# A block product scheme for the last down projection, widened from 36 to 40 of 44 input tiles and cut into two sets

## The chip, the core and the metric

The kernel runs on one core of a Trainium2 chip. The metric is device time in microseconds (us), as the median of three runs. TensorE (PE in the profile) multiplies matrices into PSUM, VectorE (DVE) and ScalarE (ACT) work element by element, GpSimd (POOL) here issues transfers that add in memory, and SyncE (SP) issues the loads of weights. PE's weight loads (PEld) run beside its matmuls.

## The reference

Two layers of an encoder over 272 tokens (16 learned ones and 256) with 2048 channels, all in float32. Each layer ends in a feed-forward block with 5632 inner channels:

```
h2 = rmsnorm(h)
up = h2 @ w_up                                     # 2048 -> 2 * 5632
act = silu(dwconv3(up[:, :5632])) * up[:, 5632:]   # conv over tokens
h  = h + act @ w_down                              # 5632 -> 2048
return h[16:]                                      # after the last layer
```

The change is in `act @ w_down` of the second layer: 256 tokens, 5632 inputs (44 tiles of 128), 2048 outputs.

## The kernel before

**Precision.** Every float32 product is made of three matmuls in a reduced form: the weights of each chunk (128 x 1024 values, 512 KB) are split by `split_w` into `wh`, a cast on ScalarE (L253), and `wl`, what the cast left out, a subtraction on VectorE (L256). Activations are split likewise (`split_to`, L1209 and L1210). Then high x high, low x high and high x low are summed in PSUM.

**The order.** `order` lists all weight chunks in the order of use. `load_raw` issues their loads on SP's queue some chunks ahead, `next_split` brings the split two chunks ahead of use (`LOOK`), and `wh` and `wl` have three buffers each. `group` (L325 to L327 for the gate half `ps_ug`, L321 and L322 for the value half `ps_uv`) multiplies one group of 256 up-projection channels: 4 chunks for the gate half, then 4 for the value half. In the last layer there are 22 such pairs of groups, 176 chunks. After each pair the code of `conv_gate` and of the loop over `UP_ORDER` makes two activation tiles on ScalarE and VectorE (L1196 to L1202, L1344 to L1347).

**The block products.** The last down projection takes `KS` = 36 of the 44 input tiles in a scheme of seven block products for eight: the tokens are cut into two halves, the 36 tiles into two halves of `NQ` = 18, the outputs into two halves of 1024. Each of the seven products `p` = 0 to 6 runs over 18 steps; one step is one weight chunk and six matmuls of 512 columns (`ps_p`, L1305). Products 3 to 6 multiply sums of weight blocks. `weight_sums` has GpSimd's queue make these sums in device memory (`ft`, L514) far ahead, four kinds one after the other over all 18 tiles. The activation operands are made by `make` into two buffers of up to three steps (`opnd`).

`PRODUCTS` fixes the order: products 0 and 4 interleaved by two steps while their activations are being made, then 5, 2, 6, 1 and 3 in full. `due` says how many of the 126 steps stand before each chunk: two steps for each pair of groups (32 in all) up to chunk 144, then 56 over the 32 up chunks of the last four group pairs, then 38 over the first 14 of the 16 tail chunks. Each product has its own pair of PSUM tiles (`open_ps`). When it is finished, `add` puts it into the result `res` in SBUF with a sign (L1271, one for each 512 columns). A sum over several products, which two parts of the output need, is kept in an SBUF tile `usum` (L1318, L1320): it starts as product 0, then products 5 and 6 are added to it.

**The tail.** The other 8 input tiles are multiplied directly: 4 output blocks of 512 (`TAIL_ORDER`), 4 chunks each, 12 matmuls of 512 columns a chunk (`ps_t`, L1379). The last block uses eighteen matmuls a chunk, six of 512 and twelve of 256 columns. Their operands are `tH` and `tL`. A counter `left` says which `add` is the last for a part of `res`; it issues the store of the output.

Of the kernel before, what the change touches and what calls it, by code (L numbers as in the profile page):

```python
# [10 lines left out]
F32 = mybir.dt.float32  # L11
# [5 lines left out]
P = 128  # L17
# [15 lines left out]
CW = 4  # L33
MG = 2
FF_SPLIT = (24, 20)
KS = 36
NQ = KS // 2
UP_ORDER = [i + j * NQ // 2 for i in range(NQ // 2) for j in range(2)] + list(range(NQ, FT // 2))
PRODUCTS = [(p, 2 * i + k) for i in range(NQ // 2) for p in (0, 4) for k in range(2)] + [(p, k) for p in (5, 2, 6, 1, 3) for k in range(NQ)]
TAIL_ORDER = (2, 3, 0, 1)  # L40
F0 = 1536

# [91 lines left out]
def encoder_kernel(ctx, tc, xT, params, consts, bmat, cfold, csign, w_fl, w_f64c, w_in, w_abr, w_four, w_f64, w_out, w_up, w_down, w_dn, w_dt, out):  # L134
# [43 lines left out]
        order.append(((1, "t", b), [(w_dt[b, j], CW) for j in range((FT - KS) // 2)]))  # L178
    prods = {0: w_dn[0, 0:NQ], 1: w_dn[0, NQ:KS], 2: w_dn[1, NQ:KS], 3: ft[3], 4: ft[0], 5: ft[1], 6: ft[2]}
    pchunks = [(prods[p][k], CW) for p, k in PRODUCTS]  # L180
    n_up, n_tail = (FT - KS) // MG * 2 * KT // CW, len(TAIL_ORDER) * (FT - KS) // 2
    n0 = 4 * (NQ // 2 - 1)
    n1 = n0 + 56
    due = lambda t: n0 + 56 * t // n_up if t <= n_up else min(n1 + (len(pchunks) - n1) * (t - n_up) // (n_tail - 2), len(pchunks))
    chunks, folded, mix, summed = [], set(), {}, {}
    t, done = 0, 0
    for key, chs in order:
        for j, ch in enumerate(chs):
            n = 0
            if key[0] == 1 and (key[1] == "t" or key[1] in ("ug", "uv") and key[2] >= KS // MG):  # L190
                n = due(t) - done
                t += 1
            elif key[0] == 1 and key[1] in ("ug", "uv") and key[2] % (NQ // 2) and j == 2:
                n = 1
            if n:
                mix[key, j] = n
                for p, k in PRODUCTS[done:done + n]:
                    if p in (3, 4, 5, 6):
                        summed[len(chunks)] = ((3, 0, 1, 2)[p - 3], k // 2)
                    chunks.append(pchunks[done])  # L200
                    done += 1
                first_mix = min(first_mix, len(chunks) - n) if done > n else len(chunks) - n
            if key[:2] == (0, "s"):
                folded.add(len(chunks))
            chunks.append(ch)
# [300 lines left out]
    def weight_sums():  # L506
        rows = lambda ap: ap.rearrange("k p c m -> (k p) (c m)")
        dst = lambda q, j: rows(ft[q, 2 * j:2 * j + 2])
        w = lambda h, k, j: rows(w_dn[h, NQ * k + 2 * j:NQ * k + 2 * j + 2])

        def issue(q, j, s, **kw):
            tick = small.tile([P, 1], F32, tag="tick", name="tick", bufs=1)
            tc.keep_in_program_order(nc.gpsimd.tensor_copy(tick, st["wl"][:, 0, 0:1].bitcast(F32)))
            tc.keep_in_program_order(nc.gpsimd.dma_start(dst(q, j), s, **kw))  # L514

        for q, base, more in ((0, lambda j: w(0, 0, j), lambda j: w(1, 0, j)),
                              (1, lambda j: dst(0, j), lambda j: w(1, 1, j)),
                              (2, lambda j: w(1, 1, j), lambda j: w(1, 0, j)),
                              (3, lambda j: w(0, 1, j), lambda j: dst(1, j))):
            for j in range(NQ // 2 + 1):  # L520
                if j < NQ // 2:
                    issue(q, j, base(j))
                    yield 1
                if j:
                    issue(q, j - 1, more(j - 1), accum_op=ALU.add, max_dma_last_dim=4096)
                    ready_sums.add((q, j - 1))
                    yield 1

    def norm_stats(holder, gap=0):
        am = small.tile([P, P // NM, NM], F32, tag="am", name="am", bufs=1)  # L530
# [28 lines left out]
    for l in range(DEPTH):  # L559
# [622 lines left out]
        with tc.tile_pool(name=f"ffn{l}", bufs=1) as fp:  # L1182
# [49 lines left out]
                slow[2] = 0  # L1232

            if last:
                KX = KS - KS // 6
                XF = XT.rearrange("p k t -> p (k t)")
                asum = XF[:, 0:NQ * P].rearrange("p (k t) -> p k t", k=NQ)
                acts = ((0, fp.tile([P, KX, SEQ], F32, name="act")),
# [8 lines left out]
                    k0, t_ = acts[k >= KX]  # L1247
                    return t_[:, k - k0:k - k0 + n, tk]

                left = {(h, b): 4 if h == 0 and b > 1 else 3 for h in range(2) for b in range(4)}  # L1250

                def to_tokens():
                    for b in range(4):
# [23 lines left out]
                def make(p, k, n):  # L1277
# [9 lines left out]
                    for q in range(n):  # L1287
                        made[p, k + q] = t_[:, 0, q], t_[:, 1, q]

                def products():  # L1290
                    usum = wp.tile([P, CW, MG * P], F32, tag="wpm", name="usum", bufs=1).rearrange("p c m -> p (c m)")
                    open_ps, late = {}, []
                    for n, (p, k) in enumerate(PRODUCTS):
                        if k == 0:
                            open_ps[p] = [psum.tile([P, 512], F32, tag="aux", name=f"ps_p{p}") for _ in range(2)]
                        ps = open_ps[p]
                        if n >= 2 * NQ - 1 and k % 3 == 1 and n + 2 < len(PRODUCTS):
                            make(*PRODUCTS[n + 2], 3)
                        if n == 2 * NQ - 2:
                            make(*PRODUCTS[2 * NQ], 3)  # L1300
                        wh, wl = (w.rearrange("p c m -> p (c m)") for w in next_split())
                        a, b = made.pop((p, k))
                        for x, w in ((a, wh), (b, wh), (a, wl)):
                            for h in range(2):
                                nc.tensor.matmul(ps[h], x, w[:, 512 * h:512 * h + 512], start=k == 0 and w is wh and x is a,  # L1305
                                                 stop=k == NQ - 1 and w is wl)
                            if x is b or w is wl:
                                step()
                                pump()
                        if late and k % 2 == 0:  # L1310
                            add(*late.pop(0))
                        if k == NQ - 1:
                            while late:
                                add(*late.pop(0))
                            for h in range(2):
                                u_ = usum[:, 512 * h:512 * h + 512]
                                if p == 0:
                                    nc.scalar.copy(u_, ps[h])  # L1318
                                if p in (5, 6):
                                    nc.vector.tensor_tensor(u_, u_, ps[h], op=ALU.add)  # L1320
                            for h in range(2):
                                u_ = usum[:, 512 * h:512 * h + 512]
                                for t_, c, minus in {0: ((0, 0, 0),), 4: ((0, 2, 0), (1, 2, 0)), 5: ((0, 2, 1),),
                                                  2: ((0, 2, 0),), 6: ((1, 0, 0), (1, 2, 1)),
                                                  1: ((0, 0, 0),), 3: ((1, 0, 0),)}[p]:
                                    late.append((t_, c + h, u_ if p in (5, 6) else ps[h], minus))
                            if p in (0, 3):
                                while late:
                                    add(*late.pop(0))
                        yield  # L1330

                st["products"] = products()
                st["pool"] = fp
                for i in UP_ORDER:
# [5 lines left out]
                    for m in range(MG):  # L1340
                        j = 2 * i + m
                        cv = cs[m][:, lo2:T]
                        v = fp.tile([P, W2], F32, tag="v", name="v", bufs=2)
                        nc.scalar.copy(v, ps[m][:, W2:2 * W2])  # L1344
                        nc.vector.tensor_tensor(v, v, ps[m][:, :W2], op=ALU.add)
                        if j < KS:
                            nc.vector.tensor_tensor(act(j, 1, slice(0, SEQ))[:, 0], cv, v, op=ALU.mult)  # L1347
                        else:
                            nc.vector.tensor_tensor(cv, cv, v, op=ALU.mult)
                            split_to(tH[:, j - KS], tL[:, j - KS], cv)  # L1350
                    if i == NQ // 2:
                        until(hold, "tokens")
                    if KS // 2 <= 2 * i < KS:
                        k1, k2 = 2 * i - NQ, 2 * i
                        a21 = act(k1, 2, tk2)
                        nc.vector.tensor_tensor(asum[:, k1:k1 + 2], a21, act(k2, 2, tk2), op=ALU.subtract)
                        nc.vector.tensor_tensor(a21, act(k1, 2, tk1), a21, op=ALU.subtract)
                        for p in (0, 4):
                            make(p, k1, 2)

                for b in TAIL_ORDER:
                    k, chs = order[st["grp"]]
# [4 lines left out]
                    ps = [psum.tile([P, 512], F32, tag="aux" if r == 2 else "mm", name=f"ps_t{r}") for r in range(len(regs))]  # L1367
# [87 lines left out]
```

## Time and profile before

| | before |
|---|---|
| median of 3 runs | 2549.21 us (2548.55 to 2549.77) |
| the profiled execution's own time | 2549.0 us |
| its span in the profile | 2547.2 us |
| PE busy | 2537.5 us (100%) |
| VectorE busy | 1785.9 us (70%) |
| ScalarE busy | 1281.3 us (50%) |
| moved by DMA | 603 MB, mean 237 GB/s |

The profile is of one execution. The span goes from its first to its last instruction; the time has 1.8 us around it. The last feed-forward block begins at about 1820 us. Times in the views are us from the start of the span, durations of single instructions in groups are ns. Matmuls are pipelined: a matmul of 512 columns lasts 390 ns from start to end, and the next starts well before that.

### The profile page before, as it was taken

What the parts mean: (1) busy time and instruction counts of PE and PEld (TensorE: products, weight loads), DVE (VectorE), ACT (ScalarE), POOL (GpSimd) and SP (SyncE); (2) the same over time, 40 slices, a digit from 0 to 9 for tenths busy, and PEclk for the clock granted to TensorE, in tenths of its full rate; (3) what the DMA queues carried; (4) which work ended last, traced back from release to release, by engine and by line L of the source; (5) the groups of instructions that cost most, each with busy time, mean ns of one, the idle gap of its engine ahead of it and who ended that gap; (6) DMA issues with size and microseconds to landing.
All of it is one profiled execution on the core that took longest, in us unless ns stands there. A gap on an engine that the chain in (4) does not pass through costs nothing.

```text
span 2547.2 us, 47579 instructions
## 1 busy us (share of the span) xinstructions
PE 2537.5 (100%) x19160; PEld 2462.4 (97%) x19160; DVE 1785.9 (70%) x2832; ACT 1281.3 (50%) x1842; POOL 86.2 (3%) x185
## 2 busy tenths in 40 slices
PE   9999999999999999999999999999999999999999
PEld 9999999999999999999999999999999999998887
DVE  7687766776666556666559787666766666678787
ACT  5455534554444334444445555444655555556665
POOL 0000000000000000000000000000000000000000
PEclk9999999999999999999999999999999999999999
DMA  6544555688898889898776546775889876668887
GB/s 237 163 155 162 187 181 183 219 245 288 292 289 274 279 285 292 271 297 266 247 226 198 175 149 189 238 216 192 277 257 300 277 241 207 205 211 271 278 297 254
DMA packets 160813, 603.01 MB, mean 237 GB/s; under 512 B 18304, under 2 KB 23552, under 8 KB 160016
## 3 DMA queue, kind: packets, MB, share of 16 engines
q1 hardware_dynamic: 148208, 522.33, 60.7%
q0 software_dynamic: 10944, 75.50, 12.3%
q8 instruction: 150, 2.46, 0.4%
q10 hardware_dynamic: 1440, 2.13, 0.2%
q14 instruction: 71, 0.58, 0.1%
HBM read 578.23 MB, written 94.37 MB: 264 GB/s over the span
## 4 chain that ended last, share of the span: by engine, by line
PE 99%; DVE 1%; DMA 0%; issue 0%; ACT 0%; SPq 0%; POOL 0%; ACTq 0%; DVEq 0%
PE ps_ug L326 7%; PE ps_p L1305 7%; PE ps_ug L327 7%; PE ps_ug L325 7%; PE ps_uv L321 6%; PE ps_d L326 3%; PE ps_uv L326 3%; PE ps_d L325 3%; PE ps_uv L327 3%; PE ps_d L327 3%; PE ps_uv L325 3%; PE ps_uv L322 3%; PE ps_o L326 2%; PE ps_gf L326 2%; PE ps_o L325 2%; PE ps_o L327 2%
## 5 line engine op out<-in xcount | busy, mean ns | idle before, releaser
L256 DVE TENSOR_TENSOR wl<-raw,wh 128x1024 fp32r<-128x1024 f32 (+1 forms) x907 | 1096.6, 1218 | 625.5 <-ACT wh L253 616.0
L253 ACT CAST wh<-raw 128x1024 fp32r<-128x1024 f32 (+1 forms) x907 | 945.9, 1047 | 951.8 <-PE ps_ug L326 170.3
L326 PE MATMUL ps_ug<-xHL,wh 128*128 128x272 f32 (+1 forms) x1408 | 402.0, 286 | 0.0
L327 PE MATMUL ps_ug<-xHL,wl 128*128 128x272 f32 (+1 forms) x1408 | 401.2, 285 | 0.0
L325 PE MATMUL ps_ug<-xHL,wh 128*128 128x272 f32 (+1 forms) x1408 | 401.0, 285 | 0.0
L325 PEld LDWEIGHTS ps_ug<-xHL,wh 128*128 128x128 f32 x1408 | 264.5, 188 | 2.2
L326 PEld LDWEIGHTS ps_ug<-xHL,wh 128*128 128x128 f32 x1408 | 264.7, 188 | 1.5
L327 PEld LDWEIGHTS ps_ug<-xHL,wl 128*128 128x128 f32 x1408 | 264.7, 188 | 0.1
L321 PE MATMUL ps_uv<-xHL,wh 128*128 128x512 f32 x704 | 249.5, 394 | 0.0
L326 PE MATMUL ps_uv<-xHL,wh 128*128 128x272 f32 x704 | 203.3, 289 | 0.0
L326 PE MATMUL ps_d<-gHL,wh 128*128 128x272 f32 x704 | 202.9, 288 | 0.0
L325 PE MATMUL ps_d<-gHL,wh 128*128 128x272 f32 x704 | 202.9, 288 | 0.0
L327 PE MATMUL ps_uv<-xHL,wl 128*128 128x272 f32 x704 | 202.6, 288 | 0.0
L325 PE MATMUL ps_uv<-xHL,wh 128*128 128x272 f32 x704 | 202.3, 287 | 0.0
L327 PE MATMUL ps_d<-gHL,wl 128*128 128x272 f32 x704 | 202.1, 287 | 0.0
L322 PE MATMUL ps_uv<-xHL,wl 128*128 128x256 f32 x704 | 198.4, 282 | 0.3 <-DVE wl L256 0.3
L321 PEld LDWEIGHTS ps_uv<-xHL,wh 128*128 128x128 f32 x704 | 132.1, 188 | 29.6
L325 PE MATMUL ps_ga<-xHL,wh 128*128 128x272 f32 (+1 forms) x512 | 147.8, 289 | 0.0
L325 PE MATMUL ps_gf<-xHL,wh 128*128 128x272 f32 (+1 forms) x512 | 146.7, 287 | 0.0
L326 PE MATMUL ps_o<-mL,wh 128*128 128x272 f32 (+1 forms) x512 | 146.5, 286 | 0.0
L327 PE MATMUL ps_o<-mH,wl 128*128 128x272 f32 (+1 forms) x512 | 146.1, 285 | 0.0
L326 PE MATMUL ps_gf<-xHL,wh 128*128 128x272 f32 (+1 forms) x512 | 146.1, 285 | 0.0
(353 smaller groups left out, 5826.7 us busy)
## 6 DMA issues: line engine op xcount, KB each, us to landing
raw<-in_w_up SPq DMA_DIRECT2D x352, 512.0 KB, 4.8
raw<-in_w_in SPq DMA_DIRECT2D x191, 512.0 KB, 3.9
raw<-in_w_down SPq DMA_DIRECT2D x88, 512.0 KB, 4.8
raw<-ft SPq DMA_DIRECT2D x72, 512.0 KB, 4.7
raw<-in_w_out SPq DMA_DIRECT2D x64, 512.0 KB, 3.6
ft<-in_w_dn POOLq DMA_DIRECT2D x27, 1024.0 KB, 11.9
raw<-in_w_dn SPq DMA_DIRECT2D x54, 512.0 KB, 4.7
raw<-in_w_abr SPq DMA_DIRECT2D x32, 512.0 KB, 3.8
```

The lines of the kernel that those rows point to most:

```text
L253: nc.scalar.copy(h[:, a:b], r[:, a:b])
L256: nc.vector.tensor_tensor(lo[:, a:b], r[:, a:b], h[:, a:b].bitcast(F32), op=ALU.subtract)
L321: nc.tensor.matmul(o2, h[:, c, sl], ab, start=kt == 0, stop=False)
L322: nc.tensor.matmul(o, lo[:, c, sl], ab[:, 0, :], start=False, stop=kt == nk - 1)
L325: nc.tensor.matmul(o, h[:, c, sl], a, start=kt == 0, stop=False)
L326: nc.tensor.matmul(o, h[:, c, sl], b, start=False, stop=False)
L327: nc.tensor.matmul(o, lo[:, c, sl], a, start=False, stop=kt == nk - 1)
L1305: nc.tensor.matmul(ps[h], x, w[:, 512 * h:512 * h + 512], start=k == 0 and w is wh and x is a, stop=k == NQ - 1 and w is wl)
```

## The change

`KS` becomes 40, in two sets of `SETS` = (12, 8) tile pairs. Each set is a complete scheme of seven products over its own tiles, one after the other: 84 steps, then 56. `HOME` says where each activation tile lies in the sets' order; `w_dn` is laid out in that order, and `weight_sums` makes all four kinds of sums for the first set and then for the second. The tail keeps 4 tiles, 2 chunks for each output block, 8 in all.

The steps stand where a written table `DUE` puts them, over all 184 chunks: none before chunk 16, 20 steps over chunks 16 to 96, 64 over 98 to 144, 12 over 144 to 160, 28 over 162 to 176, 16 over the tail chunks 176 to 182.

PSUM holds two pairs of banks, `bank`, for all products. Product 5 is accumulated on top of 0, 6 on top of both and 3 on top of these, and 2 on top of 4; only 0, 4 and 1 start afresh. After each product `add` reads the running sum, and the next product is added to it in place. So `usum` and the addition of products in SBUF go, and each product has two adds to `res`. The two pairs change roles in the second set. The last tail block's third region uses one of these banks.

Operands are made by `make_ahead`: `units` are runs of up to three steps of one product, and when a unit has been multiplied the unit two places later is made.

```diff
-KS = 36
-NQ = KS // 2
+SETS = (12, 8)
+NQ = sum(SETS)
+KS = 2 * NQ
+def _sets():
+    up, prods, home, q0 = [], [], {}, 0
+    for n in SETS:
+        up += [q0 + i + j * n // 2 for i in range(n // 2) for j in range(2)]
+        prods += [(p, q0 + 2 * i + k) for i in range(n // 2) for p in (0, 4) for k in range(2)]
+        prods += [(p, q0 + k) for p in (5, 2, 6, 1, 3) for k in range(n)]
+        for k in range(n):
+            home[2 * q0 + k], home[2 * q0 + n + k] = q0 + k, NQ + q0 + k
+        q0 += n
+    return up + list(range(NQ, FT // MG)), prods, home
+DUE = ((0, 0), (16, 0), (96, 20), (98, 20), (144, 84), (160, 96), (162, 96), (176, 124), (182, 140), (184, 140))
...
-        for q, base, more in (...):
-            for j in range(NQ // 2 + 1):
+        for q0, n in zip(FIRSTS, SETS):
+            for q, base, more in kinds:
+                j0, j1 = q0 // 2, (q0 + n) // 2
+                for j in range(j0, j1 + 1):
...
+                def make_ahead():
+                    while used[1] < min(used[0] + 2, len(units)) and whole.issuperset(units[used[1]][1]):
+                        p, qs = units[used[1]]
+                        make(p, qs[0], len(qs))
+                        used[1] += 1
...
                 def products():
-                    usum = wp.tile([P, CW, MG * P], F32, tag="wpm", name="usum", bufs=1).rearrange("p c m -> p (c m)")
...
-                        if k == 0:
-                            open_ps[p] = [psum.tile([P, 512], F32, tag="aux", name=f"ps_p{p}") for _ in range(2)]
-                        ps = open_ps[p]
-                        if n >= 2 * NQ - 1 and k % 3 == 1 and n + 2 < len(PRODUCTS):
-                            make(*PRODUCTS[n + 2], 3)
+                    bank.extend([psum.tile([P, 512], F32, tag="aux", name=f"ps_p{i}{h}") for h in range(2)] for i in range(2))
+                    for p, q in PRODUCTS:
+                        s = max(i for i, q0 in enumerate(FIRSTS) if q >= q0)
+                        ps = bank[(p in (4, 2, 1)) ^ s % 2]
+                        fresh = p in (0, 4, 1)
...
-                                nc.tensor.matmul(ps[h], x, w[:, 512 * h:512 * h + 512], start=k == 0 and w is wh and x is a,
-                                                 stop=k == NQ - 1 and w is wl)
+                                nc.tensor.matmul(ps[h], x, w[:, 512 * h:512 * h + 512], start=fresh and q in FIRSTS and w is wh and x is a,
+                                                 stop=q in LASTS and w is wl, skip_group_check=not fresh)
...
+                        if units[used[0]][1][-1] == q:
+                            used[0] += 1
+                        make_ahead()
-                        if late and k % 2 == 0:
+                        if late and q % 2 == 0:
                             add(*late.pop(0))
...
-                                if p == 0:
-                                    nc.scalar.copy(u_, ps[h])
-                                if p in (5, 6):
-                                    nc.vector.tensor_tensor(u_, u_, ps[h], op=ALU.add)
...
+                            t_, c, minus = {0: (0, 0, 0), 4: (1, 2, 0), 5: (0, 2, 1), 2: (0, 2, 0), 6: (1, 2, 1), 1: (0, 0, 0), 3: (1, 0, 0)}[p]
+                            late += [(t_, c + h, ps[h], minus) for h in range(2)]
```

More of the change, by code (lines that the diff above doesn't have):

```diff
@@ L35 @@
 FF_SPLIT = (24, 20)
-KS = 36
-NQ = KS // 2
-UP_ORDER = [i + j * NQ // 2 for i in range(NQ // 2) for j in range(2)] + list(range(NQ, FT // 2))
-PRODUCTS = [(p, 2 * i + k) for i in range(NQ // 2) for p in (0, 4) for k in range(2)] + [(p, k) for p in (5, 2, 6, 1, 3) for k in range(NQ)]
+SETS = (12, 8)
[11 more added lines that the diff above has]
+    return up + list(range(NQ, FT // MG)), prods, home
+UP_ORDER, PRODUCTS, HOME = _sets()
+FIRSTS = [sum(SETS[:i]) for i in range(len(SETS))]
+LASTS = [q + n - 1 for q, n in zip(FIRSTS, SETS)]
+DUE = ((0, 0), (16, 0), (96, 20), (98, 20), (144, 84), (160, 96), (162, 96), (176, 124), (182, 140), (184, 140))
 TAIL_ORDER = (2, 3, 0, 1)
@@ L180, in encoder_kernel, with due @@
     pchunks = [(prods[p][k], CW) for p, k in PRODUCTS]
[L181 to L184, printed above, removed]
+    def due(t):
+        (t0, d0), (t1, d1) = next(v for v in zip(DUE, DUE[1:]) if v[0][0] <= t < v[1][0])
+        return d0 + (d1 - d0) * (t - t0) // (t1 - t0)
     chunks, folded, mix, summed = [], set(), {}, {}
@@ L189, in encoder_kernel @@
             n = 0
-            if key[0] == 1 and (key[1] == "t" or key[1] in ("ug", "uv") and key[2] >= KS // MG):
+            if key[0] == 1 and key[1] in ("t", "ug", "uv"):
                 n = due(t) - done
                 t += 1
-            elif key[0] == 1 and key[1] in ("ug", "uv") and key[2] % (NQ // 2) and j == 2:
-                n = 1
             if n:
@@ L514, in issue @@
             tc.keep_in_program_order(nc.gpsimd.dma_start(dst(q, j), s, **kw))
[L516 to L519, printed above, removed]
-            for j in range(NQ // 2 + 1):
[L521 to L527, printed above, removed]
+        kinds = ((0, lambda j: w(0, 0, j), lambda j: w(1, 0, j)),
+                 (1, lambda j: dst(0, j), lambda j: w(1, 1, j)),
+                 (2, lambda j: w(1, 1, j), lambda j: w(1, 0, j)),
+                 (3, lambda j: w(0, 1, j), lambda j: dst(1, j)))
+        for q0, n in zip(FIRSTS, SETS):
+            for q, base, more in kinds:
+                j0, j1 = q0 // 2, (q0 + n) // 2
+                for j in range(j0, j1 + 1):
+                    if j < j1:
+                        issue(q, j, base(j))
+                        yield 1
+                    if j > j0:
+                        issue(q, j - 1, more(j - 1), accum_op=ALU.add, max_dma_last_dim=4096)
+                        ready_sums.add((q, j - 1))
+                        yield 1
     def norm_stats(holder, gap=0):
@@ L1234, in encoder_kernel @@
             if last:
-                KX = KS - KS // 6
+                KX = KS - 2
                 XF = XT.rearrange("p k t -> p (k t)")
@@ L1248, in act @@
                     return t_[:, k - k0:k - k0 + n, tk]
-                left = {(h, b): 4 if h == 0 and b > 1 else 3 for h in range(2) for b in range(4)}
+                left = {(h, b): (1 if h == 1 and b < 2 else 2) * len(SETS) + 1 for h in range(2) for b in range(4)}
                 def to_tokens():
@@ L1288, in make @@
                         made[p, k + q] = t_[:, 0, q], t_[:, 1, q]
-                def products():
-                    usum = wp.tile([P, CW, MG * P], F32, tag="wpm", name="usum", bufs=1).rearrange("p c m -> p (c m)")
-                    open_ps, late = {}, []
-                    for n, (p, k) in enumerate(PRODUCTS):
-                        if k == 0:
-                            open_ps[p] = [psum.tile([P, 512], F32, tag="aux", name=f"ps_p{p}") for _ in range(2)]
-                        ps = open_ps[p]
-                        if n >= 2 * NQ - 1 and k % 3 == 1 and n + 2 < len(PRODUCTS):
-                            make(*PRODUCTS[n + 2], 3)
-                        if n == 2 * NQ - 2:
-                            make(*PRODUCTS[2 * NQ], 3)
+                units = []
@@ new lines, in encoder_kernel @@
+                for n, (p, q) in enumerate(PRODUCTS):
+                    if units and units[-1][0] == p and len(units[-1][1]) < 3 and units[-1][1][-1] == q - 1:
+                        units[-1][1].append(q)
+                    else:
+                        units.append((p, [q]))
+                whole, used = set(), [0, 0]
+                def make_ahead():
[3 more added lines that the diff above has]
+                        used[1] += 1
@@ L1301, in products @@
+                bank = []
+                def products():
+                    late = []
+                    bank.extend([psum.tile([P, 512], F32, tag="aux", name=f"ps_p{i}{h}") for h in range(2)] for i in range(2))
[3 more added lines that the diff above has]
+                        fresh = p in (0, 4, 1)
                         wh, wl = (w.rearrange("p c m -> p (c m)") for w in next_split())
-                        a, b = made.pop((p, k))
+                        a, b = made.pop((p, q))
@@ L1309, in products @@
                                 pump()
-                        if late and k % 2 == 0:
+                        if units[used[0]][1][-1] == q:
+                            used[0] += 1
+                        make_ahead()
+                        if late and q % 2 == 0:
                             add(*late.pop(0))
-                        if k == NQ - 1:
+                        if q in LASTS:
                             while late:
                                 add(*late.pop(0))
-                            for h in range(2):
-                                u_ = usum[:, 512 * h:512 * h + 512]
-                                if p == 0:
-                                    nc.scalar.copy(u_, ps[h])
-                                if p in (5, 6):
[L1320 to L1326, printed above, removed]
+                            t_, c, minus = {0: (0, 0, 0), 4: (1, 2, 0), 5: (0, 2, 1), 2: (0, 2, 0), 6: (1, 2, 1), 1: (0, 0, 0), 3: (1, 0, 0)}[p]
+                            late += [(t_, c + h, ps[h], minus) for h in range(2)]
                             if p in (0, 3):
@@ L1330, in products @@
                         yield
+                    assert not late
                 st["products"] = products()
@@ L1346, in encoder_kernel @@
                         if j < KS:
-                            nc.vector.tensor_tensor(act(j, 1, slice(0, SEQ))[:, 0], cv, v, op=ALU.mult)
+                            nc.vector.tensor_tensor(act(HOME[j], 1, slice(0, SEQ))[:, 0], cv, v, op=ALU.mult)
                         else:
@@ L1350, in encoder_kernel @@
                             split_to(tH[:, j - KS], tL[:, j - KS], cv)
-                    if i == NQ // 2:
+                    if i == UP_ORDER[1]:
                         until(hold, "tokens")
-                    if KS // 2 <= 2 * i < KS:
-                        k1, k2 = 2 * i - NQ, 2 * i
+                    if NQ <= HOME.get(2 * i, 0):
+                        k2 = HOME[2 * i]
+                        k1 = k2 - NQ
                         a21 = act(k1, 2, tk2)
@@ L1357, in encoder_kernel @@
                         nc.vector.tensor_tensor(a21, act(k1, 2, tk1), a21, op=ALU.subtract)
-                        for p in (0, 4):
-                            make(p, k1, 2)
+                        whole.update((k1, k1 + 1))
+                        make_ahead()
                 for b in TAIL_ORDER:
@@ L1366, in encoder_kernel @@
                     regs = [(0, 0, 512), (1, 0, 256), (1, 256, 512)] if ends else [(0, 0, 512), (1, 0, 512)]
-                    ps = [psum.tile([P, 512], F32, tag="aux" if r == 2 else "mm", name=f"ps_t{r}") for r in range(len(regs))]
+                    ps = [psum.tile([P, 512], F32, tag="mm", name=f"ps_t{r}") if r < 2 else bank[len(SETS) % 2 == 1][0] for r in range(len(regs))]
                     for j in range(len(chs)):
@@ L1437 @@
     wd = a["w_down"][1]
-    w_dn = np.ascontiguousarray(wd[:KS * P].reshape(KS, P, 2, CW, MG * P).transpose(2, 0, 1, 3, 4))
+    w_dn = wd[:KS * P].reshape(KS, P, 2, CW, MG * P)[sorted(HOME, key=HOME.get)]
+    w_dn = np.ascontiguousarray(w_dn.transpose(2, 0, 1, 3, 4))
     w_dt = np.ascontiguousarray(wd[KS * P:].reshape(-1, 2, P, 4, 512).transpose(3, 0, 2, 1, 4).reshape(4, -1, P, CW, MG * P))
```

## The prediction

> **What bounds the kernel now.** I read the page first: engines, then the chain that ended last.
>
> ```profile
> span 2547.2 us, 47579 instructions
> PE 2537.5 (100%) x19160; PEld 2462.4 (97%) x19160; DVE 1785.9 (70%) x2832; ACT 1281.3 (50%) x1842; POOL 86.2 (3%) x185
> PEclk9999999999999999999999999999999999999999
> PE 99%; DVE 1%; DMA 0%; issue 0%; ACT 0%; SPq 0%; POOL 0%; ACTq 0%; DVEq 0%
> ```
>
> TensorE (PE) is busy all the time, at the full granted clock, and the chain is PE for 99%. So the time is the number of matmuls times what each takes of the engine, plus whatever PE waits. An instruction saved on another engine is worth nothing by itself; it matters only if that engine makes PE wait. Next I read the chain in order of time over the last stage, because it merges PE's matmuls into pieces whose length is time on the path (not the latency that the groups give for one matmul).
>
> ```profile
> 83 pieces in order of time: start us, us, what
> 2323.62 1.40 PE ps_p L1305 x6
> 2344.69 1.39 PE ps_p L1305 x6
> 2444.15 2.77 PE ps_p L1305 x12
> 2446.92 2.80 PE ps_t L1379 x12
> 2449.72 2.75 PE ps_p L1305 x12
> 2455.26 4.11 PE ps_p L1305 x18
> 2524.36 2.79 PE ps_t L1379 x18
> 2538.14 5.61 PE ps_t L1379 x36
> 2543.78 0.48 DVE res L1271
> ```
>
> The pieces follow each other without a gap: 2444.15 + 2.77 = 2446.92, where the next begins. A block product (six matmuls) costs 1.39 to 1.40 us alone, 2.75 to 2.77 for two in a row (1.38 each) and 4.11 for three (1.37 each). A chunk of the tail costs 2.80, also where its matmuls are eighteen (2.79). Then the busy time by stretches: before the dense products, in them, and in the tail (columns: the stretch, its length, then PE, PEld, DVE, ACT, POOL, the clock, the DMA share, GB/s).
>
> ```profile
> 1870.03:2277.90 407.87, 407.87 (x2754) 377.03 (x2753) 271.31 (x358) 209.47 (x272) 12.81 (x28) 1.00 0.78 243
> 2277.90:2320.60 42.70, 42.39 (x247) 36.94 (x246) 38.72 (x52) 28.43 (x38) 0.00 (x0) 1.00 0.79 259
> 2404.70:2446.80 42.10, 42.10 (x246) 37.09 (x245) 32.75 (x38) 27.06 (x35) 0.00 (x0) 1.00 0.85 275
> 2446.80:2490.00 43.20, 43.20 (x189) 35.20 (x188) 37.43 (x42) 28.30 (x32) 0.00 (x0) 1.00 0.90 309
> ```
>
> The only loss is 0.31 us in the second row, where VectorE (DVE) is 91% busy (38.72 of 42.70). So DVE is the one engine near the limit, and only where products are dense.
>
> **TensorE's work, the term that decides.** Before, 7 products of 18 steps make 126 and the tail has 4 blocks of 4 chunks, 16. After, 7 x (12 + 8) = 140 products and 4 x 2 = 8 tail chunks. The order of TensorE's instructions in both built programs gives how the products stand: before 38 alone, 28 pairs, 10 triples and two taken apart among other matmuls; after 59 alone, 33 pairs, 3 triples and six in mixed pieces.
> Before: 38 x 1.395 + 28 x 2.765 + 10 x 4.11 + 2 x 1.39 = 174.3 us. After: 59 x 1.395 + 33 x 2.765 + 3 x 4.11 + 6 x 1.39 = 194.2 us. Products add 19.9 us. The tail loses 8 x 2.80 = 22.4 us. The up projection keeps its 176 chunks. Net -2.5 us; at one mean price for a product (174.3 / 126 = 1.383) it would be 19.4 - 22.4 = -3.0. I take -2.7: between the two, as the runs get shorter, but the price by run length (1.37 to 1.40) is not known for every neighbour.
>
> **VectorE and ScalarE: more work, under cover.** These are the prices, over the whole stage 1832 to 2547 us.
>
> ```profile
> L256 DVE TENSOR_TENSOR wl<-raw,wh 128x1024 fp32r<-128x1024 f32 x312 | 375.4, 1223 | 181.9 <-ACT wh L253 180.1
> L253 ACT CAST wh<-raw 128x1024 fp32r<-128x1024 f32 x312 | 327.1, 1053 | 255.3 <-PE ps_ug L326 77.3 <-PE ps_uv L321 68.0 <-issue 57.4
> L1210 DVE TENSOR_TENSOR opnd<-XT,opnd 128x384 fp32r<-128x384 f32 x16 | 8.8, 552 | 0.0
> L1209 ACT CAST opnd<-XT 128x384 fp32r<-128x384 f32 x16 | 8.1, 509 | 0.0
> L1210 DVE TENSOR_TENSOR opnd<-act,opnd 128x256 fp32r<-128x256 f32 x9 | 3.8, 419 | 0.5 <-ACT opnd L1209 0.5
> L1271 DVE SCALAR_TENSOR_TENSOR res<-ps_p,sgn,res 128x512 f32<-128x512 f32 x12 | 8.6, 745 | 0.0
> L1271 DVE SCALAR_TENSOR_TENSOR res<-usum,sgn,res 128x512 f32<-128x512 f32 x6 | 4.4, 746 | 0.0
> L1320 DVE TENSOR_TENSOR usum<-usum,ps_p 128x512 f32<-128x512 f32 x4 | 2.6, 681 | 0.0
> ```
>
> Six more weight chunks (148 for 142) cost 6 x 1.22 = 7.3 us of DVE and 6 x 1.05 = 6.3 of ACT. Adds of products to `res` go from 18 to 28, +10 x 0.745 = 7.5; the four sums in `usum` go, -2.7; seven more small operand units, 7 x 0.42 = 2.9. DVE gets about 15 us more in a stage of 715 us where it works 515: free on average, so only the dense places count. The density in the long first part is unchanged (one product to four chunks in both). From chunk 98 to 144 it is 64 products to 46 chunks, 1.4 a chunk, where before has 14 to 8, 1.75. Denser than before is only one place: chunks 162 to 176 with two products each, while activations are still being made.
>
> ```profile
> L1196 DVE TENSOR_TENSOR u<-ps_ug,rstdB 128x258 f32<-128x258 f32 x44 | 18.6, 423 | 6.7 <-PE ps_ug L327 6.6
> L1200 DVE SCALAR_TENSOR_TENSOR cv<-u,prm,cv 128x256 f32<-128x256 f32 x44 | 21.1, 479 | 1.7 <-ACT cv L1198 1.6
> L1201 DVE SCALAR_TENSOR_TENSOR cv<-u,prm,cv 128x255 f32<-128x255 f32 x44 | 21.2, 483 | 1.3
> L1345 DVE TENSOR_TENSOR v<-v,ps_uv 128x256 f32<-128x256 f32 x44 | 18.2, 414 | 0.0
> 2363.98 0.42 DVE L1349 TENSOR_TENSOR cv<-cv,v 128x256 f32<-128x256 f32 x1
> 2364.32 1.22 DVE L256 TENSOR_TENSOR wl<-raw,wh 128x1024 fp32r<-128x1024 f32 x1
> 2365.45 0.42 DVE L1210 TENSOR_TENSOR tL<-cv,tH 128x256 fp32r<-128x256 f32 x1
> 2300.96 0.50 PE L322 MATMUL ps_uv<-xHL,wl 128*128 128x256 f32 x2 [0.31 <-DVE wl L256]
> ```
>
> PE's time there: an up chunk is (42.10 - 14 x 1.385) / 8 = 2.84, so 14 x 2.84 + 28 x 1.385 = 78.5 us. DVE: 42 subtractions x 1.22 = 51.4; 1.75 groups of eight chunks at 2 x (0.42 + 0.48 + 0.48 + 0.41 + 0.42 + 0.42) = 5.3, 9.2; 10.5 operand units x 0.55 = 5.8, and six updates of `asum` at the same 0.55, 3.3; eight adds x 0.745 = 6.0. Together 75.7, 96% by durations. But durations overlap: the subtraction at 2364.32 lasts 1.22 and the next instruction starts 1.13 later. With 0.09 off some 85 instructions it is 68 us, 87%; the same correction puts the stretch at 2277.90 (91% by durations) at about 80%, and that lost 0.31 us. The last six steps (2.67 products to a tail chunk) are as dense as the tail before (38 products over 14), which lost nothing at 87%. Bounds for the new waits: 0 (the tail row) to about 2 us (three such losses as the row at 2300.96 shows, 0.31 each, in each of two dense places); below nothing by 0.3, if that loss goes. I take no change: the first set's switch to `p` = 5, near chunk 101, has the same shape as the place of that loss.
>
> **Banks, queues, end.** The sums now stay in four banks, and PE must wait before it writes one whose add has not run. Most hand-overs have a whole block between (8 or 12 products, at least 11 us) for two adds, 1.5 us. The shortest is `p` = 0 to `p` = 5: between them lie two products of `p` = 4, and in the second set two up chunks more, 2.77 + 2 x 2.84 = 8.5 us; near chunk 101 about the same. Cost 0; if DVE ran 7 us or more behind, the wait would be what is over. On POOL's queue stand 8 more summing transfers:
>
> ```profile
> 2032.92 0.89 POOL L514 DMA_DIRECT2D ft<-ft  x1 [0.30 <-issue]
> 2045.60 0.90 POOL L514 DMA_DIRECT2D ft<-ft  x1 [0.24 <-issue]
> ```
>
> At 12.7 us a step the last moves from 2046 to 2147 us. The first load from the second set's sums stands near chunk 144, about 1832 + 144 x 2.84 + 84 x 1.39 = 2358 us, so no load on SP's queue waits for it. Three loads per 5.6 us in the densest place are fewer than in the tail row (309 GB/s). `tH` of the last group is now needed one tail chunk after its up chunks instead of three; between lie four products and a chunk, 8.3 us, for six short instructions of 0.4 us on each of two tiles: covered. The last two chunks without products (5.61 us), the final add and the output stay.
>
> Sum: 2549.0 (the profiled execution; its span is 2547.2) - 2.7, and on the median, which is 0.2 higher, **2546.5 us**, -0.11%.
>
> **Rivals.** *Operands late (slower).* An operand unit has two buffers, and `make_ahead` now issues unit n+2 right after unit n's last matmul, so ScalarE's cast, and the weight casts queued behind it, start only when PE is through, where before the buffer had been free for two products. That decides where 0.51 (cast) + 1.05 + 1.22 exceeds PE's lead of two products, 2.77 us, plus the 0.93 until `wl` is used; with one add or an evacuation between (0.75 to 1.4) it is over. If each of the 16.5 units from chunk 162 on cost its 0.51: +8.4, 2554.9 us. Against it: pairs are separated by chunks of 2.8, so the lead is mostly 4.2.
> *Bank waits.* PE could wait at hand-overs: two short ones in each set (0 to 5, and 3 to the next set's 4) at one add or two, 4 x 0.75 to 4 x 1.5: +3 to +6 on the forecast, 2549.5 to 2552.5; taken at 2549.5. In the trace of before PE never waited for an add (its one loss is the wait for `wl`), but there four buffers took turns. The Trainium skill, PSUM — Partial Sum Buffer, section PSUM bank collisions, asks that a bank be guarded as a whole against two engines at once, so TensorE can't run on in a bank while VectorE reads it; by that rule the wait exists at every hand-over, and it is free only where the add is done in time. No row here shows a sum read in the middle and then added to.
> *More gained.* The price of 1.37 belongs to the triples of the tail. If it came from the rhythm of the loads and not from the run length, all 140 products could have it: 140 x 1.37 = 191.8, +17.5 for +19.9, and with the 0.31 us of the one loss gone the sum is 17.5 - 22.4 - 0.3 = -5.2, 2544.0 us. Against it: the single products of the long first part cost 1.39 to 1.40 with DVE at 67% (271.31 of 407.87).
>
> **How the numbers follow.** Forecast 0.70 (its own range 2545.3 to 2548.0), operands late 0.12, bank waits 0.12, more gained 0.06. 0.2%, 5.1 us, is about what a measurement of this kernel can tell from no change. Faster by that (under 2544.1) is the last rival: 0.06. Slower (over 2554.3) is the upper part of operands late and some unforeseen wait: 0.11. Within: 0.83. The range takes in the forecast, the bank waits and what is near: 2544.9 to 2551.0.
>
> **What would show it.** The chain should have product pieces at 1.37 to 1.40 each and tail chunks at 2.80, PE's idle time under 1 us in the last stage, `usum` gone, and 28 adds. Operands late would show as PE waiting for `wh`, `wl` or `opnd` between 2390 and 2540 us; bank waits as PE ps_p waiting for `res` L1271. If tail chunks or products have another price, the first term is wrong.

## The result and the profile after

The changed kernel takes 2544.75 us (median of 22 runs, 2543.07 to 2547.59); the kernel before takes 2549.34 beside it (22 runs). The ratio is 0.9982 with a 95% interval of 0.9976 to 0.9989: 4.6 us less, 0.18%. The forecast was 2546.5 with a range from 2544.9 to 2551.0. The direction was right, and the gain was 4.6 us where 2.7 were forecast; the median lies 0.15 us under the range. The profiled execution took 2544.82 us, and its span is 4.2 us shorter than before.

The page first: span, engines, clock and the chain.

```profile
span 2543.0 us, 47622 instructions
PE 2532.5 (100%) x19136; PEld 2458.3 (97%) x19136; DVE 1796.0 (71%) x2851; ACT 1283.3 (50%) x1849; POOL 94.1 (4%) x201
PEclk9999999999999999999999999999999999999999
PE 98%; DVE 1%; DMA 0%; issue 0%; ACT 0%; SPq 0%; POOL 0%; ACTq 0%; DVEq 0%
```

TensorE has 24 matmuls fewer (108 fewer in the tail, 84 more in the products) and is still the chain. Then the chain's last part, in order of time (start, length, what).

```profile
2486.80 2.77 PE ps_p L1336 x12
...
2495.15 2.80 PE ps_t L1405 x12
2497.95 2.75 PE ps_p L1336 x12
2500.70 2.80 PE ps_t L1405 x12
2503.50 4.11 PE ps_p L1336 x18
...
2539.51 0.48 DVE res L1290
```

The prices are those of before: 2.77 and 2.75 for two products, 4.11 for three, 2.80 for a tail chunk. The last add starts at 2539.51, in the kernel before at 2543.78. The waits of TensorE and of its weight loads from 1860 us on have one row:

```profile
PEld ps_uv L338 <- DVE wl L272: 0.2, 1, 0.2
```

Before, that place had a loss on PE itself (0.31 us by its row). VectorE in the two dense places, chunks 162 to 176 and then the tail (columns as in the prediction's view of stretches):

```profile
2410.90:2495.00 84.10, 84.10 (x490) 74.02 (x489) 72.40 (x93) 55.24 (x72) 0.00 (x0) 1.00 0.80 271
2495.00:2533.70 38.70, 38.70 (x169) 31.55 (x168) 35.84 (x41) 24.74 (x28) 0.00 (x0) 1.00 0.81 288
```

It is 86% and 93% busy, and PE is busy without a gap.

For what follows I add up the time from each matmul's start to the next one's, by tile, over the last stage (from the first `ps_ug` matmul to the start of the last tail matmul; the third region of the last tail block is counted as tail). The sums contain every wait of PE.

| us | `ps_ug` | `ps_uv` | products | tail | others | stage |
|---|---|---|---|---|---|---|
| before | 253.09 | 247.41 | 174.63 | 44.63 | 3.35 | 723.10 |
| changed | 252.52 | 246.94 | 193.56 | 22.26 | 3.35 | 718.62 |
| difference | -0.57 | -0.47 | +18.93 | -22.37 | 0 | -4.48 |

So the two large terms were nearly those of the prediction (+19.9, -22.4). The gain is 2.0 us larger than their sum of -2.5: 1.0 us lies in the up chunks (`ps_ug`, `ps_uv`), which it had left unchanged, and 1.0 us in the products.

### The profile page after: what moved, and what is told of

Its sections match the earlier page's. It is cut to its first block, busy times and chain, and to the rows that moved or that the text cites. A ratio compares the mean times of both kernels' runs of the same rounds, so it can differ in the third digit from the quotient of the medians.

```text
span 2543.0 us, 47622 instructions
## 1 busy us (share of the span) xinstructions
PE 2532.5 (100%) x19136; PEld 2458.3 (97%) x19136; DVE 1796.0 (71%) x2851; ACT 1283.3 (50%) x1849; POOL 94.1 (4%) x201
## 4 chain that ended last, share of the span: by engine, by line
PE 98%; DVE 1%; DMA 0%; issue 0%; ACT 0%; SPq 0%; POOL 0%; ACTq 0%; DVEq 0%
PE ps_p L1336 8%; PE ps_ug L342 7%; PE ps_ug L343 7%; PE ps_ug L341 7%; PE ps_uv L337 6%; PE ps_d L342 3%; PE ps_uv L342 3%; PE ps_d L341 3%; PE ps_uv L343 3%; PE ps_d L343 3%; PE ps_uv L341 3%; PE ps_uv L338 3%; PE ps_o L342 2%; PE ps_gf L342 2%; PE ps_o L341 2%; PE ps_o L343 2%
## 5 line engine op out<-in xcount | busy, mean ns | idle before, releaser
L1336 PE MATMUL ps_p<-wh,opnd 128*128 128x512 f32 x560 | 152.7, 394 | 0.0
```

## The experiments

Each expectation stood before its run. "Stage" is the time of the table above.

**The kernel before, profiled again.** No edit.

> The kernel before, profiled once more, to see how well the length of the last stage repeats (from the start of its first ps_ug matmul to the start of the last tail matmul: 723.1 us before, 718.6 after). If the order of TensorE's instructions and prices per matmul set it, 723.1 within 0.2 us and the one loss of 0.3 to 0.6 us near the switch to product 5 comes again; if the 4.5 us are scatter between executions, it comes out up to some us away.

The stage is 723.10 us again, with the same five sums to 0.01 us, though the whole execution took 2553.52 us. The `ps_ug` rows of the last layer in the two profiles (min/median/max duration, first and last start) show where the 4.5 us lie:

```profile
L325 PE MATMUL ps_ug<-xHL,wh x704: 277/282/483, 1820.4 to 2422.7; 128*128 128x258 f32 x176
L325 PE MATMUL ps_ug<-xHL,wh x704: 277/282/482, 1824.9 to 2427.2; 128*128 128x258 f32 x176
```

The stage begins 4.5 us later, and ends as much later. Matched matmul by matmul, the shift is complete at 51.4 us of the first profile. So the stage can repeat closely where whole times scatter by some us. It does not always do so: the second profile of the changed kernel, below, is 1.35 us longer than its first. Most of the experiments rest on one profile each.

**Single products between groups in the kernel before.**

```diff
-    t, done = 0, 0
+    t, done, u = 0, 0, 0
...
-            elif key[0] == 1 and key[1] in ("ug", "uv") and key[2] % (NQ // 2) and j == 2:
-                n = 1
+            elif key[0] == 1 and key[1] in ("ug", "uv"):
+                n = int(u > 16 and u % 4 == 0)
+                u += 1
```

> The kernel before with its 32 single products two chunks later, so that they stand between two groups and not in the middle of one; nothing else is changed. Theory A (where a single product stands sets a part of the price: between groups, product and up chunks together cost about 0.04 us less): the stage gets 32 x 0.04 = 1.3 us shorter, 721.8. Rival B (the cheaper up chunks of the changed kernel come from its lighter schedule or its sums in PSUM, not from the place): no change, 723.1.

Stage 721.8 us (252.40, 247.01, 174.44, 44.63): 1.3 less, as theory A said. The place counts.

**Single products in mid-group in the changed kernel.**

```diff
-DUE = ((0, 0), (16, 0), (96, 20), (98, 20), (144, 84), ...
+DUE = ((0, 0), (18, 0), (98, 20), (144, 84), ...
```

> The changed kernel with its 20 single products of the first part two chunks later, in the middle of a group instead of between two groups; all else as in the changed kernel. Theory A (place sets part of the price): 20 x 0.04 = 0.8 us longer, 719.4. Rival B (the place does not matter): 718.6.

Stage 719.4 us (252.95, 247.19, 193.68, 22.26): 0.8 more, theory A again. In the chain the period of eight up chunks and two products can be read off directly. Two starts of like pieces for each kernel: before, single products moved, changed, changed with products in mid-group.

```profile
2028.90 1.40 PE ps_p L1305 x6
2054.40 1.40 PE ps_p L1305 x6
```

```profile
2009.75 1.39 PE ps_p L1306 x6
2035.16 1.39 PE ps_p L1306 x6
```

```profile
2008.96 1.39 PE ps_p L1336 x6
2034.38 1.38 PE ps_p L1336 x6
```

```profile
2002.70 1.39 PE ps_p L1336 x6
2028.20 1.40 PE ps_p L1336 x6
```

25.50 and 25.50 us with the products in mid-group, 25.41 and 25.42 between groups, whichever kernel it is. It is no matter of single waits: from 1895 to 2120 us every whole `ps_ug` group between two products takes 11.435 us in edge36 and in the changed kernel, where two halves with a product between them take 11.48 on the mean (2 x 5.74) in the kernel before and in mid20. For `ps_uv` it is 11.204 and 11.23.

**The new machinery at the old width.**

```diff
-SETS = (12, 8)
-DUE = (...)
-KX = KS - 2
+SETS = (18,)
+DUE = ((0, 0), (14, 0), (142, 32), (144, 32), (176, 88), (190, 126), (192, 126))
+KX = KS - 6
```

> The changed kernel with one set of 36 tiles and the schedule of the kernel before: as many products and tail chunks as before, in the same places, with the running sums in PSUM and the operands made by make_ahead. Theory A (the sums in PSUM and make_ahead lie under cover; they only can take away the one loss at the switch to product 5): 723.1 or, without that loss, 722.5. Rival B (they save time on TensorE's path of themselves): 721 or less. Rival C (operands late, of the prediction): over 724, with PE waiting for wh, wl or opnd.

Stage 723.1 us, with the same product sum, 174.63. The sums in PSUM and `make_ahead` gain nothing of themselves, and the loss at the switch to product 5 is still there:

```profile
PE ps_uv L338 <- DVE wl L272: 0.3, 1, 0.3
PEld ps_uv L338 <- DVE wl L272: 0.9, 2, 0.8
PEld ps_p L1336 <- ACT wh L269: 0.2, 1, 0.2
```

So what took the loss away is the schedule. It has 1.4 products to a chunk there and not 1.75, but that the lower density is the reason is not shown: the version with one set, below, has four to a chunk and no row of a wait of PE.

**Sums back in SBUF, at the new width.** The kernel's `usum` and its own PSUM tiles for each product are put back into `products`:

```diff
-                        ps = bank[(p in (4, 2, 1)) ^ s % 2]
+                        if q in FIRSTS:
+                            open_ps[p] = [psum.tile([P, 512], F32, tag="aux", name=f"ps_p{p}") for _ in range(2)]
+                        ps = open_ps[p]
...
+                                if p == 0:
+                                    nc.scalar.copy(u_, ps[h])
+                                if p in (5, 6):
+                                    nc.vector.tensor_tensor(u_, u_, ps[h], op=ALU.add)
```

> The changed kernel with its running sums back in usum as before (each product in PSUM tiles of its own, 18 adds to res a set, two copies on ScalarE and four sums on VectorE a set). Theory A (the sums in PSUM are off TensorE's path): the last stage stays at 718.6 us, VectorE does 8 x 0.745 + 8 x 0.68 = 11.4 us more. Rival B (the lighter work at the switches is what took the loss of 0.6 away, or VectorE is near its limit in chunks 162 to 176): 719.2 or more, with PE waiting for wl.

Stage 718.8 us, 0.2 more, all of it one wait in the tail (22.48 for 22.26):

```profile
PEld ps_t L1416 <- DVE wl L272: 0.4, 1, 0.4
PEld ps_uv L338 <- DVE wl L272: 0.2, 1, 0.2
```

Theory A, with a small price for VectorE's 11 us more (536.7 us busy from 1832 us on, for 526.0). The sums in PSUM are worth 0.2 us by this one profile.

**One set of 40 tiles.**

```diff
-SETS = (12, 8)
-DUE = (...)
+SETS = (20,)
+DUE = ((0, 0), (16, 0), (160, 36), (176, 100), (182, 140), (184, 140))
```

> The changed kernel with one set of 20 tile pairs: the same 140 products and 8 tail chunks, but only 36 products before chunk 160, then four to a chunk and 6.7 to a tail chunk. VectorE's durations: 5 x 1.22 + 0.66 + 1.1 + 0.4 = 8.3 us for 2.84 + 4 x 1.37 = 8.3 us of PE. Theory A (what counts is the durations less the 0.09 us overlap each, 92%): PE waits little, 718 to 721. Rival B (operands late, of the prediction: the lead of two chunks is not enough in runs of four and more products): each of the 22 dense steps loses 0.5 us, 729 or more.

Stage 717.8 us, under the changed kernel. Runs of four products to a chunk and of six or seven to a tail chunk cost 1.37 each (5.49 for four). Its two dense stretches:

```profile
2328.00:2461.90 133.90, 133.90 (x707) 114.59 (x706) 121.51 (x146) 96.81 (x121) 0.00 (x0) 1.00 0.88 309
2461.90:2533.00 71.10, 71.10 (x312) 58.21 (x311) 67.22 (x72) 52.60 (x59) 0.00 (x0) 1.00 0.91 337
```

VectorE is busy for 91% and 95% of them, and the four waits of PE's weight loads for `wl` are 0.2 to 0.3 us each. Cutting the scheme into two sets is not what gains here. Timed beside the changed kernel:

> The kernel with one set of 20 tile pairs once more, timed beside the changed kernel. Its last stage was 717.8 us in one profile against 718.6 for two sets. If the stage is all that differs: the median about 0.8 us under that of the changed kernel, 5.3 us (0.21%) under the kernel before; a rival, that the one profile was lucky in its waits: equal to the changed kernel or slower, with a stage of 719 or more.

> The changed kernel on the same chip and beside the same runs of the kernel before. Its stage should be 718.6 us again (within 0.2), as the stage of the kernel before came out the same to 0.1 us in two profiles, and the median 4.5 us under the kernel before.

One set: 2543.78 us (11 runs), ratio 0.9980 (0.9971 to 0.9988), stage 717.8 again. The changed kernel: 2545.55 us (11 runs), ratio 0.9986 (0.9977 to 0.9995). The kernel before: 2548.98 (21 runs). One set is the fastest version, though its interval overlaps that of two sets. Of the 1.8 us between the two medians the stages of the first profiles show 0.8. The changed kernel's stage came out at 720.0 in this profile, not at the 718.6 that was expected; 1.2 of the 1.35 us are in `ps_ug` at one place, 2165 us, and 0.1 in the product before it. The waits there:

```profile
ACT wh L269 <- DMA raw<-ft: 3.2, 3, 2.8
PEld ps_ug L343 <- DVE wl L272: 1.2, 1, 1.2
PE ps_ug L343 <- DVE wl L272: 1.0, 1, 1.0
```

A cast waited for a load of a weight sum, so VectorE's subtraction was late, so PE waited. From 2134 to 2170 us, the kernel before and this profile of the changed one:

```profile
2134.00:2170.00 36.00, 36.00 (x243) 33.20 (x242) 22.76 (x31) 18.81 (x25) 0.00 (x0) 1.00 0.65 207
2134.00:2170.00 36.00, 35.03 (x209) 30.71 (x208) 28.87 (x37) 21.06 (x26) 2.94 (x4) 1.00 0.97 299
```

The DMA share is 0.97 where it was 0.65: the last summing transfers (the last is issued at 2151 us here, at 2148 in the first profile) lie beside the first dense products.

**Summing transfers earlier.**

```diff
-                slow[2] = (18 if last else 24) if last or half else 0
+                slow[2] = (13 if last else 24) if last or half else 0
```

> The changed kernel with its summing transfers in the last layer issued every 13 steps instead of 18, so that the last of them is out well before the products get dense at chunk 98 (about 2134 us). If the late loads there come from the summing transfers beside the denser loads: from 2134 to 2170 us the DMA share falls from 0.97 to about 0.85, loads land in 4 to 5 us (6.7 and 7.7 in the two profiles of the changed kernel) and no cast waits for a load of ft; the stage is 718.6. If the loads alone are too dense there: landing stays at 6 to 8 us.

The last transfer is issued at 2037 us, the stage is 718.6, and no cast waits for a load there. The stretch, and the time from issue to landing of the loads issued in it (with the earlier transfers, then in the first and in the second profile of the changed kernel):

```profile
2134.00:2170.00 36.00, 36.00 (x215) 31.85 (x214) 30.03 (x39) 22.09 (x28) 0.00 (x0) 1.00 0.77 253
```

```profile
DMA to landing us min/median/max: 3.3/4.7/5.2
```

```profile
DMA to landing us min/median/max: 4.3/7.5/10.5
DMA to landing us min/median/max: 4.5/8.4/11.9
```

So it is the summing transfers that make the loads late, in both profiles of the changed kernel. That this costs PE 1.35 us is seen in one of the two only.

**All products between groups.** `DUE` is written as steps: five or six products at each edge between groups from chunk 100 to 144, three to chunk 160, seven from 164 to 176.

> The changed kernel with all products from chunk 98 to 176 put between groups: runs of five or six there, three to chunk 160, seven from 164 on; as many in all. Theory A (place sets part of the price, and two chunks of lead suffice): products at 1.37 in runs and cheaper up chunks, 0.5 to 1.5 us shorter, 717.1 to 718.1. Rival B (operands late): runs of five to seven products lose 0.5 to 1 us each, 12 + 4 of them, 724 or more, with waits for wh, wl or opnd.

Stage 724.9 us, rival B in size, though not by late operands. Waits of PE and of its weight loads, the smaller ones left out:

```profile
PE ps_uv L338 <- DVE wl L272: 0.9, 2, 0.5
PE ps_p L1336 <- DVE wl L272: 0.7, 2, 0.4
PEld ps_uv L338 <- DVE wl L272: 4.4, 9, 1.0
PEld ps_p L1336 <- DVE wl L272: 4.1, 10, 0.8
PEld ps_ug L343 <- DVE wl L272: 1.1, 3, 0.4
PEld ps_p L1336 <- DVE res L1290: 0.5, 1, 0.5
PEld ps_p L1336 <- DVE opnd L1229: 0.2, 1, 0.2
```

What is late is `wl`, hardly ever the operand. Over 2126 to 2500 us VectorE is only 78% busy (292.23 of 374.00); in the changed kernel, where PE does not wait, it is 80% (298.68). Evenly spread runs of four (one set) at 91% lost less too. So the mean share does not decide here, the rhythm does. A run of up to seven products at the edge meets the making of the activations, which VectorE has to do at that moment too; that this meeting is the reason is argued, not shown by a run.

**Pairs at one kind of edge.** The 20 first products as ten pairs, all between a value half and the next gate half.

> The changed kernel with its 20 first products as ten pairs, each between the value half of one group and the gate half of the next; none between gate and value half. If the gain of the place comes from the edge value to gate alone (0.043 us for each gate half, half of it at this edge in the sums before): ps_ug stays at 252.5, ps_uv goes back from 246.9 to 247.2, stage 718.9. If both edges carry their own part in the same way: ps_ug 252.7, ps_uv 247.1, stage 719.0. If it is only how many runs there are: 719.0 with ps_p a little cheaper.

Stage 718.95 us (252.83, 246.99, 193.52, 22.26). `ps_uv` keeps about four fifths of its gain (246.94 in the changed kernel, 247.19 in mid-group), though no product stands before a value half; `ps_ug` keeps a quarter to a third (252.52 and 252.95). None of the three guesses fits both. Which edge carries which part, and what makes the same matmuls dearer on the mean (0.044 us on the 96 of a `ps_ug` group), stays open.

## Why the prediction was wrong by its own steps

**TensorE's work: the mechanism held, the sum was off in three terms.** The tail's 22.4 us came out as 22.37. The products were priced by run length, +19.9; measured +18.93. Of the difference 0.5 is the loss that sat in the products of before. At before's mean without it, (174.63 - 0.48) / 126 = 1.382, fourteen more are 19.35, and mid20 shows 193.68 - 174.15 = 19.5. So shorter runs cost next to nothing, and 0.4 us of my surcharge was not there.

**The loss at the switch was left in, and it went.** I took no change because the switch looked alike in both. It is worth 0.6 us, not the 0.31 of its row: from the matmuls' starts, the six of that product took 1.87 us for 1.39 and the chunk around it 2.91 for 2.80. psum36 kept it with the schedule of before, mid20 lost it, and usum40 lost it with the sums back in SBUF (products 193.53): so the new schedule removed it. Which feature of the schedule did stays open. The lower density is not shown to be it, as one40 with four products to a chunk has no row of a wait of PE.

**The missing term is the place of single products.** Here the prediction failed most: I kept "176 chunks" at one price. In the changed kernel the singles stand between groups: -0.43 in `ps_ug`, -0.25 in `ps_uv`, -0.12 in the products, together -0.8 us, turned on and off in both kernels (edge36, mid20). The profile of before could show only the 25.50 us of the two periods, since that kernel puts none of its single products between groups. A further 0.36 in the up chunks is left between the kernel before and mid20. Of this 0.10 is the loss's share; 0.26 is not assigned.

Summed: -22.37 (tail) + 19.35 (products) + 0.18 (what mid20's 19.53 is above that) - 0.58 (loss) - 0.80 (place) - 0.26 (not assigned) = -4.48, as measured. My range let the gain grow only by 1.6 us, as if errors in the 3520 up-chunk matmuls could not add; 0.3 ns on each is 1 us.

**VectorE and the operands: right.** VectorE did not make PE wait in chunks 162 to 176, at 86% (96% by the sum of durations was forecast and 87% after the overlap). The forecast of 15 us more work was right: by the sum of durations from 1832 us on it is 558.0 us for 543.2. The page's 10 us (1796.0 for 1785.9) count overlapping time once. One reading was wrong, though: the busy time of the stretches has the overlap taken out already. The one at 2277.90 is 41.7 us by durations, 98%, and 91% after the overlap; my 80% took it out twice. So the forecast 87% stood nearer to the place with the loss than I wrote. `make_ahead` cost nothing (psum36), and one40 ran with runs of six and seven in the tail.

**Banks: right.** 28 adds of 0.74 us, and no row of a wait of PE or of its weight loads for them. The wait for an add, which I had weighed, showed in the bursts alone, as 0.5 us of a weight load waiting for `res` and 0.2 us of PE. The bank rule behind it (the Trainium skill, PSUM — Partial Sum Buffer, PSUM bank collisions) asks that a bank be guarded as a whole; the trace agrees that this was free where the add was done in time, and no run here leaves the guard out.

**Queues: wrong in a way that did not decide.** No load waited for its own sum, as said. But I compared bandwidth only at chunks 162 to 176 and in the tail, and not where the eight more transfers meet the dense products, chunks 99 to 107: there loads took 7.5 and 8.4 us, and 4.7 with the transfers out of the way, with a cost of 0 or 1.35 us by execution.

**Rivals.** Operands late and bank waits did not happen. "More gained" had the right size for a wrong reason: products did not fall to 1.37 here (they do in one40, 192.42 / 140 = 1.374).

## What to carry to other kernels

Where one engine is the whole chain, count its instructions by the price of pieces on the path and forecast that; then ask what small price each of the many untouched instructions would have to change by to matter, and put that into the range. Read the length of the changed stage from the trace, not only whole times: here it repeated to 0.1 us in the kernel before and with one set, while executions differ by up to 5. But take it twice, as the changed kernel's own stage came out 1.35 us apart. Work that feeds the bound engine should be spread evenly; and when a side stream (here the summing transfers) is made longer, look at what it newly runs beside, not only at when it is needed.

## What was not expected of the hardware

Whole times scatter by the start: over all profiles, in which TensorE has the same work up to there, the last stage began between 1819.5 and 1824.9 us. The two profiles of the kernel before show what the 4.5 us are. A wait of PE at 48 us makes 1.4 of them; the other 3.1 grow while the granted clock is at half, by the clock's record from 49.0 to 55.8 us of the second profile. The stretch from 48 to 56 us, in the first profile and in the second (the clock is the third number from the end):

```profile
48.00:56.00 8.00, 8.00 (x67) 8.00 (x67) 6.35 (x21) 3.19 (x8) 0.00 (x0) 1.00 0.39 121
48.00:56.00 8.00, 6.93 (x32) 6.96 (x33) 5.26 (x22) 1.25 (x5) 0.00 (x0) 0.57 0.39 133
```

All four profiles whose last stage began after 1823 us have such a stretch (6.8 us long in this one, 3.4 in the others), and none of the other nine has one before the kernel's end. Why the clock falls there is open.

And the mean price of the same matmuls depends a little on their neighbours: eight up chunks and two products took 25.41 or 25.50 us by the place of the products alone, with no wait shown in either.
